# Stacked parts for the new tokens, and query/key operands made for a pair of heads: one change to a decoder-step kernel

## The chip, the core and the metric

The kernel runs on one core of one Trainium2 chip, as one program. The metric is the device time of one execution in microseconds (us), smaller is better; the figure of a kernel is the median of several executions. Engines are named as the profile names them: PE is TensorE's matmul stream and PEld its weight loads, DVE is VectorE, ACT is ScalarE, POOL is GpSimd, SP is SyncE, whose queue issues nearly all transfers.

## What is computed

One inference step of a two-layer hybrid decoder, in float32, for a prompt of 512 tokens and 64 "new" tokens (8 samples with 8 tokens each and 1024 cached keys each).

```
layer 0:  qa,ka,va,qi,ki,wi,qb,kb,vb,fb = split(h @ w_in)        # h: 512 + 64 rows of 1024
          A: per-query top-k keys by an indexer, softmax over them      (8 heads of 64)
          B: softmax with a forget gate: s + cum[t] - cum[s], causal    (8 heads of 64)
          x = LN(ALPHA*x + (1+g1) * (concat(A,B) @ w_out))
layer 1:  u, v = split(gelu(h @ w_in_c)); x = LN(ALPHA*x + (1+g1) * ((u * (W_s LN(v) + b)) @ w_out_c))
each:     h = x*(1+scale)+shift;  x = LN(ALPHA*x + (1+g2) * ConvFFN(h))
```

The prompt attends to itself; each sample attends to its cached pages, found through a page table, and to its own 8 new rows.

## The kernel before

**Split operands.** Products are made at float32 precision from float32r operands: a value is split into a high part (rounded, suffix `h`) and a low part (what is left, suffix `l`), and `mm3` adds the three products high-high, high-low and low-high. `split_to` makes a pair: a cast on ACT, then a subtraction on DVE. `weights` (L250 to L254) loads a unit of 128 x 1024 weights as `wr`, casts it to `wh` on ACT and subtracts to `wl` on DVE or POOL.

**Token-major projections.** `token_unit` computes rows of tokens times a unit of weights: for each block of 128 prompt tokens by three products (L283 to L285), and for the block of 64 new tokens (`tb` = 4) by a single plain float32 product per 128 rows of the model dimension, `xn` against the unsplit weight `wr` (L702). Even and odd `k` go into the lower and upper 64 partitions of one accumulator, and `both_halves` (L717 ACT, L718 DVE) adds the two halves. This code serves `w_ab` (2 projections, 8 units, 512 columns a product), `w_aa` (3 projections, 12 units, 256 columns) and the v half of the gMLP, `w_v` (16 units, 256 columns). `xn` is made in `modulate` (L430, a POOL copy per 128 features) for layer 0 and in `Norm.finish` (L144, L146) for the gMLP.

**Attention of the prompt.** `attend_prompt` goes through 8 heads of B and then 8 of A; a head has four steps `tb`, one for each block of 128 queries: scores (L1265, L1266, for B also L1268), softmax (`softmax`, L1201 to L1204), transposes (L1273), and a copy out (L1274). After the second head of a pair, eight products with the values follow (L1282). `operands` makes what a head needs: `qS` (scaled query; partitions 0 to 63 hold the high part, 64 to 127 the low part), `kH` and `kL` (the key's parts, twice, so that one product adds two), for B also `cq`. It loads the 64 rows of one head twice, into the lower and the upper half of a tile called `both` (L1220 for B, L1226 for A; A's rows are token-major and go through four transposes a tile, L1229). The operands of the next head are asked for at step `TA` = 1 of the present one; there are two buffers of each (`QB`), and three of `both` (`TWB`).

**What sets the order.** The code asks for the work in the order above, interleaved with generators: in the attention stage the heads advance by 1.2 steps for each step of `attend_sample`, which loads two pages at a time (L269) into the weight buffers and multiplies them (L1329 scores, L1363 values). A scheduler then places each instruction in its engine's queue. Queues run in order; SP's queue holds the page loads, the loads of `both` and `rows`, and 128 loads of page numbers (L277).

**Stages of the traced execution:** layer 0 projections with the first sample attention (0 to 366 us), attention of the prompt with the rest of the sample attention (366 to 578), output projection and ConvFFN (to about 1121), gMLP with its v projection first (1121 to 1235), the rest of layer 1.

Of the kernel before, what the change touches and what calls it, by code (L numbers as in the profile page):

```python
# [48 lines left out]
LB = 'gv'  # L49
TWB = 3  # L50
BP = 200
# [4 lines left out]
GO = (((0,4),(4,8),(8,12)),((12,16),))  # L56
QB = 2


class Norm:  # L60
# [56 lines left out]
    def finish(self, part):  # L117
# [19 lines left out]
        if part:  # L137
            ps = psum.tile([P, KB, NS], F32, name="tp", bufs=2)
            for kb in range(KB):
                nc.tensor.transpose(ps[:, kb], rt[:NS, 4, kb * P:(kb + 1) * P], ident[:NS, :NS])  # L140
            self.xn = xp.tile([P, KB, NS], F32, name="xn")
            t = self.xn.rearrange("p k (b q) -> p k b q", b=8)
            wide = lambda m: m[:, :, :, None].to_broadcast([P, KB, 8, 8])
            nc.vector.tensor_tensor(t, ps.rearrange("p k (b q) -> p k b q", b=8), wide(self.gains), op=OP.mult)  # L144
            nc.scalar.copy(x[:, :, NP:], ps)
            nc.vector.tensor_tensor(t, t, wide(self.offs), op=OP.add)  # L146
            net.split_to(*(w[:, :, NP:] for w in self.out), self.xn)
        for k0 in range(0, KB, 2):
            ks = slice(k0, k0 + 2)
# [53 lines left out]
class Net:  # L203
# [217 lines left out]
    def modulate(self, xk, sc1, sh, kb, pool):  # L421
# [126 lines left out]
    def gmlp(self, x, last, psum, pool, xp, *norm):  # L548

        nc, a, xs, xn = self.nc, self.a, last.xs, last.xn  # L550
        g1 = self.plus_one(1, 2, xp, "g1")
# [21 lines left out]
        def lead():  # L573
            c, u = todo.pop(0)
            if u == 0:
                led[c] = [], [psum.tile([P, 2, 256], F32, name=name, bufs=b) for name, b in (("acc", 4), ("tc", 2))]
            units, accs = led[c]
            units.append(self.weights(a["w_v"][c, u], 1024))
            self.token_unit({tb: accs[tb // 4][:, tb % 2] for tb in (2, 3, 4)}, units[u], u, 256, xs, xn, True, (2, 3, 4))

# [3 lines left out]
        for c in range(8):  # L584
            first = None
            for u in range(2):
# [3 lines left out]
                first = first or psum.tile([P, 2, 256], F32, name="acc", bufs=4)  # L590
                self.token_unit([first[:, 0], first[:, 1]], units[u], u, 256, xs, xn, True, (0, 1))
            accs = [first] + led.pop(c)[1]
# [91 lines left out]

    def token_unit(self, accs, w, u, n, xs, xn, shared=False, tbs=range(5), between=None):

# [4 lines left out]
        for tb in tbs:  # L691
            for j in range(per):
# [14 lines left out]
    def token_product(self, accs, srcs, xs, xn, n, between=None, shared=False, before=None):  # L707

        for u, src in enumerate(srcs):
            w = self.weights(src, 1024)  # L710
            if before:
                before(u)
            self.token_unit(accs, w, u, n, xs, xn, shared, between=between)

# [55 lines left out]
    def project(self, keep, pool, room, psum, free):  # L770
# [5 lines left out]
        xs = self.xs = [self.halves(tuple(x[:, kb] for x in self.xhl)) for kb in range(KB)]  # L776
        self.xn = pool.tile([P, KB, NS], F32, name="xn")
        self.sc1 = pool.tile([P, KB, 9], F32, name="sc1")
# [56 lines left out]
        toks = self.five(psum)  # L835
        self.token_product(toks, [a["w_ab"][0, u] for u in range(4)], xs, self.xn, 512, None, False, before)
        qit = self.pair(tmp, [P, 4, NP], "qit")
# [5 lines left out]
        kd = tmp.tile([P, 5, P], F32, name="kd")  # L843
        rt = tmp.tile([P, 5, 64], F32, name="rt8")
        for n, t0, t1 in ((P, 0, 4), (NS, 4, 5)):
# [18 lines left out]
        for ci, name in enumerate(("qi", "vb")):  # L864
            accs = toks
            if ci:
                accs = self.five(psum)
                self.token_product(accs, [a["w_ab"][ci, u] for u in range(4)], xs, self.xn, 512, between)
            for tb in range(5):
# [50 lines left out]
    def project_a(self, pool, psum, xs, between):  # L920
# [3 lines left out]
        for c, name in enumerate(("va", "ka", "qa")):  # L924
            for half in range(2):
                cols = slice(256 * half, 256 * half + 256)
                accs = [psum.tile([P, 2, 256], F32, name="s", bufs=5) for _ in range(3)]
                self.token_product([accs[tb // 2][:, tb % 2] for tb in range(5)], [a["w_aa"][c, half, u] for u in range(2)],
                                   xs, self.xn, 256, between, True)
                for i in range(3):  # L930
# [275 lines left out]

    def operands(self, kind, h, hm, pool, psum):

        nc = self.nc
        hp, par = h // 2, h % 2
        qs, kh, kl = (pool.tile([P, NP], F32R, name=n, bufs=QB) for n in ("qS", "kH", "kL"))
        low = slice(64, P)
        for c in "qk":
            t = pool.tile([P, NP], F32, name="both", bufs=TWB)
            src = self.qkv[c + kind]
            if kind == "b":
                for d in range(2):
                    nc.sync.dma_start(t[64 * d:64 * d + 64], src[hp, 64 * par:64 * par + 64])  # L1220
            else:

                rows = t.rearrange("p (t d n) -> p t d n", t=4, d=2)
                src = src.rearrange("(t p) n -> p t n", p=P)[:, :, 64 * h:64 * h + 64]
                for d in range(2):
                    nc.sync.dma_start(rows[:, :, d], src)  # L1226
                t = psum.tile([P, NP], F32, name="tp", bufs=2)
                for tb in range(4):
                    nc.tensor.transpose(t[:, tb * P:(tb + 1) * P], rows[:, tb].rearrange("p d n -> p (d n)"), self.ident)  # L1229
# [5 lines left out]
        cq = v = None  # L1235
        if kind == "b":
            cq = pool.tile([P, NP], F32R, name="cq", bufs=QB)
            nc.gpsimd.tensor_scalar(cq, self.cumq[h // 4].bitcast(F32), hm[:, h % 4:h % 4 + 1], None, op0=OP.mult)
        if par == 0:
            v = pool.tile([P, NP], F32, name="rows", bufs=2).rearrange("p (t n) -> p t n", t=4)  # L1240
            nc.sync.dma_start(v, self.qkv["v" + kind].rearrange("(t p) n -> p t n", p=P)[:, :, hp * P:hp * P + P])
        return qs, kh, kl, cq, v

    def attend_prompt(self, mt, pool, ptp, psum, flush):
# [3 lines left out]
        heads = [(kind, h) for kind in "ba" for h in range(8)]  # L1248
        ahead = [self.operands(*heads[0], hm, pool, psum)]
        for i, (kind, h) in enumerate(heads):  # L1250
# [3 lines left out]
            first = 0 if kind == "a" else 4  # L1254
            qs, kh, kl, cq, v = ahead.pop()
# [378 lines left out]
```

## Time and profile before

| | |
|---|---|
| median of 3 executions | 1940.66 us (1937.17 to 1941.69) |
| profiled execution, own time | 1944.53 us |
| its span | 1942.8 us |
| busy: PE, PEld, DVE, ACT, POOL | 94%, 84%, 60%, 38%, 18% |
| mean granted TensorE clock | 0.97 of full |
| transfers | 283.36 MB, 146 GB/s over the span |

The span is the time from the first to the last instruction; 1.7 us of the execution lie around it. A busy share is an average over stages with different limits; in PE's row of the 40 slices the digits are 8 and 9 nearly everywhere, and the DMA row has 5 to 9 in slices 4 to 12, which end with the attention of the prompt, and at most 5 after them.

### The profile page before, as it was taken

What the parts mean: (1) busy time and instruction counts of PE and PEld (TensorE: products, weight loads), DVE (VectorE), ACT (ScalarE), POOL (GpSimd) and SP (SyncE); (2) the same over time, 40 slices, a digit from 0 to 9 for tenths busy, and PEclk for the clock granted to TensorE, in tenths of its full rate; (3) what the DMA queues carried; (4) which work ended last, traced back from release to release, by engine and by line L of the source; (5) the groups of instructions that cost most, each with busy time, mean ns of one, the idle gap of its engine ahead of it and who ended that gap; (6) DMA issues with size and microseconds to landing.
All of it is one profiled execution on the core that took longest, in us unless ns stands there. A gap on an engine that the chain in (4) does not pass through costs nothing. (4 is left out here: it accounts for less than half of the span.)

```text
span 1942.8 us, 37068 instructions
## 1 busy us (share of the span) xinstructions
PE 1826.5 (94%) x14460; PEld 1622.8 (84%) x14460; DVE 1157.8 (60%) x2426; ACT 743.7 (38%) x1382; POOL 351.3 (18%) x518
## 2 busy tenths in 40 slices
PE   6889999899889899999999999999998999999996
PEld 4647877655459799999999989999997999999995
DVE  2549963465448754545556963465577655555577
ACT  2323222255443542424345432422234535344543
POOL 2323511110015310101012330110013101010124
PEclk9989999999899999999999999999998999999997
DMA  8346577797874335353543422332132222213242
GB/s 288 127 155 219 179 253 244 241 307 232 266 240 149 116 131 189 135 161 135 195 141 107 131 92 78 97 97 59 63 112 72 78 97 67 97 56 108 87 139 92
DMA packets 140865, 283.36 MB, mean 146 GB/s; under 512 B 32722, under 2 KB 43922, under 8 KB 140690
## 3 DMA queue, kind: packets, MB, share of 16 engines
q1 hardware_dynamic: 139970, 278.64, 43.9%
q0 software_dynamic: 720, 2.36, 0.5%
q8 instruction: 114, 1.87, 0.4%
q14 instruction: 61, 0.50, 0.1%
HBM read 270.00 MB, written 10.94 MB: 145 GB/s over the span
## 5 line engine op out<-in xcount | busy, mean ns | idle before, releaser
L298 PE MATMUL acc<-xl,wh 128*128 128x256 f32 (+1 forms) x1664 | 496.2, 298 | 5.9 <-DVE xl L162 5.9
L298 PE MATMUL acc<-xh,wh 128*128 128x256 f32 (+1 forms) x1664 | 498.6, 300 | 2.9 <-ACT xh L161 1.7
L298 PE MATMUL acc<-xh,wl 128*128 128x256 f32 (+1 forms) x1664 | 495.0, 298 | 0.0
L251 ACT CAST wh<-wr 128x1024 fp32r<-128x1024 f32 (+2 forms) x276 | 260.7, 949 | 537.3 <-PE acc L298 375.3
L254 DVE TENSOR_TENSOR wl<-wr,wh 128x1024 fp32r<-128x1024 f32 (+2 forms) x211 | 226.7, 1076 | 248.0 <-ACT wh L251 222.4
L298 PEld LDWEIGHTS acc<-xh,wh 128*128 128x128 f32 x1664 | 318.2, 191 | 11.7 <-issue 6.4
L298 PEld LDWEIGHTS acc<-xl,wh 128*128 128x128 f32 x1664 | 318.5, 191 | 7.5 <-DVE xl L162 7.1
L298 PEld LDWEIGHTS acc<-xh,wl 128*128 128x128 f32 x1664 | 318.5, 191 | 0.4 <-issue 0.4
L254 POOL TENSOR_TENSOR wl<-wr,wh 128x1024 fp32r<-128x1024 f32 x65 | 160.9, 2476 | 526.6 <-ACT wh L251 471.8
L298 PE MATMUL acc<-gl,wh 128*128 128x256 f32 (+1 forms) x704 | 209.5, 299 | 0.0
L298 PE MATMUL acc<-gh,wl 128*128 128x256 f32 (+1 forms) x704 | 207.8, 298 | 1.6 <-DVE wl L254 1.6
L298 PE MATMUL acc<-gh,wh 128*128 128x256 f32 (+1 forms) x704 | 208.2, 301 | 0.4 <-ACT gh L760 0.4
L439 DVE SCALAR_TENSOR_TENSOR x<-acc,g,x 128x256 f32<-128x256 f32 x256 | 119.7, 476 | 116.9 <-PE acc L298 111.5
L525 DVE SCALAR_TENSOR_TENSOR y<-up,wc,y 128x592 f32<-128x592 f32 x176 | 150.6, 856 | 34.0 <-ACT y L522 30.0
L298 PEld LDWEIGHTS acc<-gh,wh 128*128 128x128 f32 x704 | 132.9, 190 | 5.5 <-ACT wh L251 2.1
L298 PEld LDWEIGHTS acc<-gh,wl 128*128 128x128 f32 x704 | 132.8, 190 | 2.9 <-DVE wl L254 1.9
L298 PEld LDWEIGHTS acc<-gl,wh 128*128 128x128 f32 x704 | 133.9, 190 | 0.3 <-DVE gl L761 0.2
L518 POOL COPY tail<-up 128x2 f32<-128x2 f32 x88 | 26.3, 299 | 519.1 <-ACT up L516 518.8
L516 ACT COPY up<-acc 128x256 f32<-128x256 f32 x176 | 65.2, 371 | 129.9 <-PE acc L298 121.7
L283 PE MATMUL s<-wh,xh 128*128 128x256 f32 (+1 forms) x256 | 81.7, 327 | 1.4 <-ACT wh L251 1.4
L522 ACT ACTIVATE y<-up,wc 128x592 f32<-128x592 f32 x88 | 77.8, 884 | 9.2 <-POOL up L514 1.1
L285 PE MATMUL s<-wh,xl 128*128 128x256 f32 (+1 forms) x256 | 81.3, 317 | 0.0
(442 smaller groups left out, 3468.3 us busy)
## 6 DMA issues: line engine op xcount, KB each, us to landing
wr<-in_w_up SPq DMA_DIRECT2D x88, 512.0 KB
wr<-in_w_down SPq DMA_DIRECT2D x32, 512.0 KB
wh<-in_w_mod SPq DMA_DIRECT2D x30, 512.0 KB
wl<-in_w_mod SPq DMA_DIRECT2D x30, 512.0 KB
wr<-in_w_mod SPq DMA_DIRECT2D x28, 512.0 KB
own<-in_kT_b SPq DMA_DIRECT2D x48, 256.0 KB
own<-in_v_b SPq DMA_DIRECT2D x44, 256.0 KB
wr<-in_w_down SPq DMA_DIRECT2D x32, 320.0 KB
```

Of the source, the lines that this page charges most:

```text
L251: nc.scalar.copy(h, r)
L254: (nc.vector if low == "v" else nc.gpsimd).tensor_sub(l, r, h.bitcast(F32))
L283: mm(out, sh, mh, start=start, stop=False)
L285: mm(out, sl, mh, start=False, stop=stop)
L298: mm(acc, w[:, k * P:(k + 1) * P], m, start=i == 0, stop=i == n - 1)
L439: nc.vector.scalar_tensor_tensor(xp, acc[:, :256], g1[:, ob, 0:1], xp, op0=OP.mult, op1=OP.add)
L516: nc.scalar.copy(u[:, 2 + 256 * part:258 + 256 * part], accs[part][:, :256])
L518: nc.gpsimd.tensor_copy(tail[:, blk, 0:2], u[:, NP:NP + 2])
L522: nc.scalar.activation(y[:, :n], u[:, 0:n], AF.Identity, bias=wc[:, 3, blk:blk + 1], scale=wc[:, 0, blk:blk + 1])
L525: nc.vector.scalar_tensor_tensor(y[:, :n], u[:, k:k + n], wc[:, k, blk:blk + 1], y[:, :n], op0=OP.mult, op1=OP.add)
```

## The change

Two edits, and some buffer counts.

1. **New tokens.** `xn` is replaced by `xst`, which holds for each `k` the high and the low part of the 64 new tokens side by side, 128 columns in all. A product with `wh` and one with `wl` (L707 of the new file) replace the plain product with `wr`: partitions 0 to 63 of the accumulator collect the high rows, 64 to 127 the low rows, and `both_halves` adds them as it did. `xst` is filled by POOL copies from the split operands: two per 128 features in `modulate`, and two of 128 x 512 in each of the three norms that have a next layer (only the one before the gMLP is read).
2. **Operands by pair.** `operands` is called once for a pair of heads, at step 0 of the pair's second head. It loads the 128 rows of both heads once for the query and once for the key, transposes them once (A), and then makes each head's `qS`, `kH` and `kL` from 64 rows at a time. `QB` is 3, `TWB` is 2.

```diff
-        nc.gpsimd.tensor_copy(self.xn[:, kb], t[:, NP:])
         self.split_to(*(x[:, kb] for x in self.xhl), t)
+        for i, x in enumerate(self.xhl):
+            nc.gpsimd.tensor_copy(self.xst[:, kb, i], x[:, kb, NP:])
...
             net.split_to(*(w[:, :, NP:] for w in self.out), self.xn)
+            self.xst = xp.tile([P, KB, 2, NS], F32R, name="xst")
+            for i, w in enumerate(self.out):
+                nc.gpsimd.tensor_copy(self.xst[:, :, i], w[:, :, NP:])
...
-                    c = 64 * (k % 2)
-                    self.nc.tensor.matmul(accs[tb][c:c + NS], xn[:, k], wk[2], start=k < 2, stop=k >= KB - 2,
-                                          tile_position=(0, c))
+                    x = xst[:, k].rearrange("p i n -> p (i n)")
+                    for i in range(2):
+                        self.nc.tensor.matmul(accs[tb], x, wk[i], start=k + i == 0, stop=k + i == KB)
...
-            if kind == "b":
-                for d in range(2):
-                    nc.sync.dma_start(t[64 * d:64 * d + 64], src[hp, 64 * par:64 * par + 64])
+            if kind == "b":
+                nc.sync.dma_start(t, src[hp])
             else:
-                rows = t.rearrange("p (t d n) -> p t d n", t=4, d=2)
-                src = src.rearrange("(t p) n -> p t n", p=P)[:, :, 64 * h:64 * h + 64]
-                for d in range(2):
-                    nc.sync.dma_start(rows[:, :, d], src)
+                rows = t.rearrange("p (t n) -> p t n", t=4)
+                nc.sync.dma_start(rows, src.rearrange("(t p) n -> p t n", p=P)[:, :, hp * P:hp * P + P])
...
-            if c == "q":
-                nc.scalar.activation(qs, t, AF.Copy, scale=0.125)
-                nc.vector.scalar_tensor_tensor(qs[low], t[low], 0.125, qs[low].bitcast(F32), op0=OP.mult, op1=OP.subtract)
-            else:
-                self.split_to(kh, kl, t)
+        for (qs, kh, kl), own in zip(ops, halves):
+            nc.scalar.activation(qs[:64], tq[own], AF.Copy, scale=0.125)
+            nc.vector.scalar_tensor_tensor(qs[low], tq[own], 0.125, qs[:64].bitcast(F32), op0=OP.mult, op1=OP.subtract)
+            for half in halves:
+                nc.scalar.copy(kh[half], tk[own])
+                nc.vector.tensor_sub(kl[half], tk[own], kh[half].bitcast(F32))
...
-                if tb == TA and i < 15:
-                    ahead.append(self.operands(*heads[i + 1], hm, pool, psum))
+                if tb == 0 and par and i < 15:
+                    kind2, h2 = heads[i + 1]
+                    ahead += self.operands(kind2, h2 // 2, hm, pool, psum)
```

The order moves at three places that matter below. Line numbers of the new file are 3 to 6 higher for the same code.

PE before, at the end of one unit of the gMLP's v projection (`acc` are prompt tokens, `tc` holds the new tokens):

```order
L284 MATMUL acc<-wl,xh 128x256
L285 MATMUL acc<-wh,xl 128x256
L702 MATMUL tc<-wr,xn 64x256 x4
L283 MATMUL acc<-wh,xh 128x256
L284 MATMUL acc<-wl,xh 128x256
```

and PE now, at the same place:

```order
L287 MATMUL acc<-wl,xh 128x256
L288 MATMUL acc<-wh,xl 128x256
L707 MATMUL tc<-wh,xst 128x256
L707 MATMUL tc<-wl,xst 128x256
L707 MATMUL tc<-wh,xst 128x256
L707 MATMUL tc<-wl,xst 128x256
L707 MATMUL tc<-wh,xst 128x256
L707 MATMUL tc<-wl,xst 128x256
L707 MATMUL tc<-wh,xst 128x256
L707 MATMUL tc<-wl,xst 128x256
L286 MATMUL acc<-wh,xh 128x256
L287 MATMUL acc<-wl,xh 128x256
```

Four plain products become eight float32r products, in the same place between the same neighbours.

DVE before, early in the A heads, ahead of a `mtl` (the low part of a pair's result; `selp` is the mask of the selected keys, `p` the probabilities, `mx` the sample attention's maximum):

```order
L1201 ISA p,nm<-s,selp_1223 128x512
L1201 ISA nm 128x1
L1203 RECIPROCAL sm<-sm 128x1
L1204 TENSOR_SCALAR p<-p,sm 128x384
L1232 SCALAR_TENSOR_TENSOR qS<-tp,qS 64x512
L1203 RECIPROCAL sm<-sm 128x1
L1204 TENSOR_SCALAR p<-p,sm 128x512
L761 TENSOR_TENSOR mtl<-o,mth 128x512
```

and DVE now, around the same `mtl`:

```order
L1208 TENSOR_SCALAR p<-p,sm 128x384
L1235 SCALAR_TENSOR_TENSOR qS<-tp,qS 64x512
L1338 TENSOR_REDUCE mx<-s 128x1
L1238 TENSOR_TENSOR kL<-tp,kH 64x512
L1235 SCALAR_TENSOR_TENSOR qS<-tp,qS 64x512
L1238 TENSOR_TENSOR kL<-tp,kH 64x512
L765 TENSOR_TENSOR mtl<-o,mth 128x512
L1238 TENSOR_TENSOR kL<-tp,kH 64x512
L1338 TENSOR_REDUCE mx<-s 128x1
L1205 ISA p,nm<-s,selp_1245 128x512
L1205 ISA nm 128x1
L1238 TENSOR_TENSOR kL<-tp,kH 64x512
```

The softmax over four blocks (128x512) stood ahead of the operand instruction there; now five of a pair's six operand instructions stand ahead of it.

SP before, at the first operands of the attention stage (`d_qb`, `o_bk_p`, `o_bv_p` are the stored queries, keys and values of B):

```order
L1220 DMA both<-d_qb 64x512 x2
L1220 DMA both<-o_bk_p 64x512 x2
L1241 DMA rows<-o_bv_p 128x4x128
L944 DMA d_qa<-ro 128x2x256
L1220 DMA both<-d_qb 64x512 x2
```

and SP now:

```order
L1224 DMA both<-d_qb 128x512
L1224 DMA both<-o_bk_p 128x512
L1246 DMA rows<-o_bv_p 128x4x128 x2
L1224 DMA both<-d_qb 128x512
```

Pairs of half-tile loads become single loads; the first of them now stands behind ten further page loads (eight of keys, two of values) that stood after it.

## Rows read from the trace of the kernel before

**Rows 1.** Windows: PE, PEld, DVE, ACT, POOL busy; PEclk, DMA share, GB/s

```profile
300.00:372.00 72.00, 64.56 (x710) 50.71 (x708) 25.32 (x62) 14.72 (x35) 11.03 (x9) 0.95 0.72 236
...
366.00:578.00 212.00, 177.47 (x1712) 106.58 (x1704) 110.27 (x372) 104.19 (x294) 19.75 (x18) 0.92 0.85 261
...
1121.00:1235.00 114.00, 113.45 (x891) 101.07 (x892) 53.92 (x108) 37.35 (x60) 15.68 (x13) 0.99 0.29 95
```

**Rows 2.** Timeline of PE in the gMLP: start us, duration us, instruction

```profile
1181.92 0.28 PE L284 MATMUL acc<-wl,xh 128*128 128x256 f32 x1
1182.04 0.28 PE L285 MATMUL acc<-wh,xl 128*128 128x256 f32 x1
1182.25 1.08 PE L702 MATMUL tc<-wr,xn 128*64 128x256 f32 x8
...
1183.49 0.28 PE L284 MATMUL acc<-wl,xh 128*128 128x256 f32 x1
```

**Rows 3.** Timeline of PE around one unit of `w_ab`

```profile
59.78 0.39 PE L284 MATMUL s<-wl,xh 128*128 128x512 f32 x1
60.02 0.40 PE L285 MATMUL s<-wh,xl 128*128 128x512 f32 x1
60.34 1.08 PE L702 MATMUL s<-wr,xn 128*64 128x512 f32 x4
61.35 0.35 PE L283 MATMUL tp<-xh,cums 128*80 128x256 f32 x1
```

**Rows 4.** Timeline of PE around one unit of `w_aa`

```profile
364.75 1.08 PE L702 MATMUL s<-wr,xn 128*64 128x256 f32 x8
365.76 0.64 PE L1363 MATMUL o<-wr,ptS 128*32 128x128 f32 x16
```

**Rows 5.** Source L430 (ns min/median/max, starts), and a POOL timeline row

```profile
L430 POOL COPY xn<-tmp x8: 237/238/239, 14.6 to 59.0; 128x64 f32<-128x64 f32 x8
...
94.09 0.54 POOL L1016 MEMSET rt<- 128x512 f32 x1
```

**Rows 6.** Timelines of POOL and DVE at the norm before the gMLP

```profile
1108.37 2.40 POOL L254 TENSOR_TENSOR wl<-wr,wh 128x1024 fp32r<-128x1024 f32 x1 [3.33 <-ACT wh L251]
...
1108.85 2.47 DVE L162 TENSOR_TENSOR xl<-tmp,xh 128x512 fp32r<-128x512 f32 x1
...
1122.64 0.68 DVE L162 TENSOR_TENSOR xl<-tmp,xh 128x512 fp32r<-128x512 f32 x1
```

**Rows 7.** Timeline of PE: transposes of one A head's operands

```profile
459.20 1.09 PE L1229 MATMUL tp<-c_ident,both 128*128 128x128 f32 x8
460.22 0.62 PE L1329 MATMUL s<-wl,qbda 128*32 128x256 f32 x2
```

**Rows 8.** Waits of PE, 372 to 580 us: total us, times, longest

```profile
PE tp L1353 <- ACT pS L1344: 6.5, 4, 2.1
PE s L1329 <- DMA wr<-in_kT_a: 5.7, 3, 3.7
PE s L1265 <- DVE qS L1232: 2.9, 1, 2.9
PE s L1329 <- DMA wh<-in_kT_a: 2.3, 1, 2.3
```

**Rows 9.** Lines, 366 to 578 us: busy us, mean ns | idle before, releaser

```profile
L1232 DVE SCALAR_TENSOR_TENSOR qS<-both,qS 64x512 fp32r<-64x512 f32 x8 | 5.9, 736 | 4.3 <-ACT qS L1231 4.0
L761 DVE TENSOR_TENSOR kL<-tp,kH 128x512 fp32r<-128x512 f32 x8 | 5.5, 690 | 2.7 <-ACT kH L760 2.7
...
L760 ACT CAST kH<-both 128x512 fp32r<-128x512 f32 x8 | 4.9, 619 | 7.2 <-DMA both<-o_bk_p 6.9 <-PE s L1266 0.3
```

**Rows 10.** Transfers of 370 to 580 us, and one of the issue rows

```profile
DMA packets 47615, 54.38 MB, mean 259 GB/s; under 512 B 20087, under 2 KB 24439, under 8 KB 47588
...
both<-d_qa SPq DMA_DIRECT2D x16, 128.0 KB
```

**Rows 11.** Issue of the loads of `both` on SP: ns min/median/max

```profile
L1220 SPq DMA_DIRECT2D both<-d_qb x16: 451/460/1287, 366.4 to 425.4; - x16
```

More of the change, by code (lines that the diff above doesn't have):

```diff
@@ L548, in gmlp @@
     def gmlp(self, x, last, psum, pool, xp, *norm):
-        nc, a, xs, xn = self.nc, self.a, last.xs, last.xn
+        nc, a, xs, xst = self.nc, self.a, last.xs, last.xst
         g1 = self.plus_one(1, 2, xp, "g1")
@@ L578, in lead @@
             units.append(self.weights(a["w_v"][c, u], 1024))
-            self.token_unit({tb: accs[tb // 4][:, tb % 2] for tb in (2, 3, 4)}, units[u], u, 256, xs, xn, True, (2, 3, 4))
+            self.token_unit({tb: accs[tb // 4][:, tb % 2] for tb in (2, 3, 4)}, units[u], u, 256, xs, xst, True, (2, 3, 4))
         for _ in range(3):
@@ L590, in gmlp @@
                 first = first or psum.tile([P, 2, 256], F32, name="acc", bufs=4)
-                self.token_unit([first[:, 0], first[:, 1]], units[u], u, 256, xs, xn, True, (0, 1))
+                self.token_unit([first[:, 0], first[:, 1]], units[u], u, 256, xs, xst, True, (0, 1))
             accs = [first] + led.pop(c)[1]
@@ L683, in rows, with token_unit @@
         return bass.AP(tensor=ap.tensor, offset=ap.offset, ap=[[0, n]] + [list(s) for s in ap.ap[1:]])
-    def token_unit(self, accs, w, u, n, xs, xn, shared=False, tbs=range(5), between=None):
+    def token_unit(self, accs, w, u, n, xs, xst, shared=False, tbs=range(5), between=None):
         per = 1024 // n
@@ L712, in token_product @@
                 before(u)
-            self.token_unit(accs, w, u, n, xs, xn, shared, between=between)
+            self.token_unit(accs, w, u, n, xs, xst, shared, between=between)
     def both_halves(self, acc, out):
@@ L776, in project @@
         xs = self.xs = [self.halves(tuple(x[:, kb] for x in self.xhl)) for kb in range(KB)]
-        self.xn = pool.tile([P, KB, NS], F32, name="xn")
+        self.xst = pool.tile([P, KB, 2, NS], F32R, name="xst")
         self.sc1 = pool.tile([P, KB, 9], F32, name="sc1")
@@ L835, in project @@
         toks = self.five(psum)
-        self.token_product(toks, [a["w_ab"][0, u] for u in range(4)], xs, self.xn, 512, None, False, before)
+        self.token_product(toks, [a["w_ab"][0, u] for u in range(4)], xs, self.xst, 512, None, False, before)
         qit = self.pair(tmp, [P, 4, NP], "qit")
@@ L867, in project @@
                 accs = self.five(psum)
-                self.token_product(accs, [a["w_ab"][ci, u] for u in range(4)], xs, self.xn, 512, between)
+                self.token_product(accs, [a["w_ab"][ci, u] for u in range(4)], xs, self.xst, 512, between)
             for tb in range(5):
@@ L928, in project_a @@
                 self.token_product([accs[tb // 2][:, tb % 2] for tb in range(5)], [a["w_aa"][c, half, u] for u in range(2)],
-                                   xs, self.xn, 256, between, True)
+                                   xs, self.xst, 256, between, True)
                 for i in range(3):
@@ L1205, in softmax, with operands @@
         return p
-    def operands(self, kind, h, hm, pool, psum):
+    def operands(self, kind, hp, hm, pool, psum):
         nc = self.nc
-        hp, par = h // 2, h % 2
-        qs, kh, kl = (pool.tile([P, NP], F32R, name=n, bufs=QB) for n in ("qS", "kH", "kL"))
         low = slice(64, P)
+        halves = [slice(64 * par, 64 * par + 64) for par in range(2)]
+        ops = [tuple(pool.tile([P, NP], F32R, name=n, bufs=QB) for n in ("qS", "kH", "kL")) for _ in range(2)]
+        both = []
         for c in "qk":
@@ L1235, in operands @@
-        cq = v = None
-        if kind == "b":
[L1237 to L1242, printed above, removed]
+                    nc.tensor.transpose(t[:, tb * P:(tb + 1) * P], rows[:, tb], self.ident)
@@ new lines, in operands @@
+            both.append(t)
+        tq, tk = both
+        for (qs, kh, kl), own in zip(ops, halves):
[4 more added lines that the diff above has]
+                nc.vector.tensor_sub(kl[half], tk[own], kh[half].bitcast(F32))
+        cqs = [None, None]
+        if kind == "b":
+            for par in range(2):
+                h = 2 * hp + par
+                cqs[par] = pool.tile([P, NP], F32R, name="cq", bufs=QB)
+                nc.gpsimd.tensor_scalar(cqs[par], self.cumq[h // 4].bitcast(F32), hm[:, h % 4:h % 4 + 1], None, op0=OP.mult)
@@ L1244, in attend_prompt @@
+        v = pool.tile([P, NP], F32, name="rows", bufs=2).rearrange("p (t n) -> p t n", t=4)
+        nc.sync.dma_start(v, self.qkv["v" + kind].rearrange("(t p) n -> p t n", p=P)[:, :, hp * P:hp * P + P])
+        return [(*op, cq, v) for op, cq in zip(ops, cqs)]
     def attend_prompt(self, mt, pool, ptp, psum, flush):
@@ L1248, in attend_prompt @@
         heads = [(kind, h) for kind in "ba" for h in range(8)]
-        ahead = [self.operands(*heads[0], hm, pool, psum)]
+        ahead = self.operands("b", 0, hm, pool, psum)
         for i, (kind, h) in enumerate(heads):
@@ L1254, in attend_prompt @@
             first = 0 if kind == "a" else 4
-            qs, kh, kl, cq, v = ahead.pop()
+            qs, kh, kl, cq, v = ahead.pop(0)
             if par == 0:
```

9 lines of the change are left out of this document (4 added, 5 removed).

## Prediction

> **What bounds the kernel now.** I read the busy line and the 40 slices first: PE is busy 94% of the span, so the first question for each edit is how much PE time it takes away, and the second is where PE is not full. The windows answer it [rows 1]. In the gMLP's v projection (1121 to 1235 us) PE is busy 113.45 of 114 us, and the transfers use 0.29 of their time: whatever PE saves there shortens the execution. At the end of the layer 0 projections (300 to 372 us) PE is busy 64.56 of 72 us, or 0.90. In the attention of the prompt (366 to 578 us) it is busy 177.47 of 212 us; the transfers are at 0.85, DVE and ACT at about half. There no engine is full: 34.5 us of PE are idle. The list of waits [rows 8] says for what: pages of the sample attention (5.7 and 2.3 us), its softmax (6.5 us), and once the first operands (2.9 us). The rest is in many small waits. So the new-token edit is a sum of PE durations, and the pair edit is a question of which of four half-loaded resources sets the pace.
>
> **New tokens, gMLP.** In the timeline [rows 2] the float32r products start 0.12 us apart (1181.92, 1182.04). From the last of these before the plain products to the second after them (1182.04 to 1183.49) 1.45 us pass, of which two steps of 0.12 would be spent without the plain ones: they cost 1.21 us a unit. The order puts eight float32r products of the same 128x256 shape in their place, 8 x 0.12 = 0.96 us. That saves 0.25 us in each of 16 units, 4.0 us, all of it on a full PE.
>
> **New tokens, layer 0.** For `w_ab` [rows 3] a step of 512 columns takes 0.24 us (59.78 to 60.02), and from 60.02 to 61.35 1.33 us pass: 1.09 us for the plain products, against 4 x 0.24 = 0.96 now. 8 units save 1.0 us. For `w_aa` between products of the sample attention [rows 4] the plain ones take 1.01 us and save 0.05; between float32r neighbours, as in rows 2, they save 0.25. Most of the 12 units stand between such neighbours in both orders, so I take 0.2: 2.4 us. PE was 0.90 busy there, so of 3.4 us I count 3.0; bounds are 0 (a wait fills it) and 4.0 (12 at 0.25, and 1.0).
>
> **New tokens, the copies.** `xst` adds 8 POOL copies to the first 8, 0.24 us each [rows 5], and they now wait for the low part, one DVE instruction later. POOL's weight subtractions are queued behind them, 8 x 0.24 = 1.9 us at most. At the three norms there are two copies of 128x512 each; the trace has none, the nearest row of that size is a fill of 0.54 us [rows 5]. Six of them are 3.2 us of POOL, which is busy for 18% of the span. I take +0.5 us, since PE has other products at both places; bounds 0 and +5.1.
>
> Here the trace has something that speaks against the change: beside a POOL subtraction of 2.40 us a DVE subtraction took 2.47 us, and 0.68 us when POOL was idle [rows 6]. The Trainium skill's "SBUF — State Buffer", section "Who interferes with whom", says that a VectorE instruction with two SBUF inputs and a GpSimd instruction that reads SBUF exclude each other for the whole instruction; the row agrees. By that rule each norm copy may hold DVE for its own length, and the sum would carry +3.2 instead of +0.5, 2.7 us more than I forecast. I keep +0.5, since in the norms PE has other products to do while DVE catches up.
>
> **Pair operands, PE.** The eight transposes of an A head take 1.02 us (459.20 to 460.22) [rows 7]. Eight heads need 64, four pairs need 32: 4.1 us of PE less. PE is 84% busy in this stage, so this could also vanish in idle time; bounds 0 and -4.1, I take all of it, since the transposes stand among the sample attention's products, which are ready.
>
> **Pair operands, transfers and SP.** In 370 to 580 us 54.38 MB move at 259 GB/s [rows 10], and 60 loads of `both` of 128 KB (16 and 16 for A, 14 and 14 for B) are 7.9 MB of it. A pair's load is half of that: 3.9 MB less, 15 us of transfer at that rate. On SP 60 issues of about 0.46 us [rows 11] become 15 or 16, so some 20 us of the queue go too, and page loads stand behind fewer others. Not all of that is time: PE waits for pages 8.0 us by the two longest rows [rows 8]. I take three quarters of it, -6 us. Bounds: 0 (the pages wait for buffers that PE frees, and none comes sooner) and -15. Against it, SP now issues the first operands behind ten more page loads: 128x512 floats each, 2.6 MB in all, 10 us at 259 GB/s if the products that come first can't use the wait. Those pages are wanted by the products beside them, so I count nothing; the first wait of 2.9 us [rows 8] may double.
>
> **Pair operands, ACT and DVE.** An instruction on 64 partitions takes as long as one on 128 (0.74 us for the `qS` subtraction on 64, 0.69 us for `kL` on 128, [rows 9]). A head had two casts on ACT and two subtractions on DVE; now it has three of each. Over 16 heads that is 16 x 0.62 = 9.9 us of ACT and 16 x 0.70 = 11.2 us of DVE, on engines with about 100 us idle in the stage. They come bunched: six on DVE for a pair, 4.2 us, where two of 1.4 us in all stood before, and a softmax of the running head stands behind them, and behind that its transposes on PE. Bounds: 0, and 8 pairs x 2.8 = 22 us if every bunch is exposed. PE has the sample attention to do meanwhile, so I take +2.5.
>
> **Buffers.** With `QB` = 3 the next pair needs two sets while the present second head holds one, so no operand waits for a buffer; `both` at 2 holds one pair's query and key, freed about 13 us (four steps of 212/64 us) ahead of the next use. I count nothing.
>
> **Sum.** -4.0 - 3.0 + 0.5 - 4.1 - 6 + 2.5 = -14.1 us. Against the profiled execution's own 1944.53 us (its span of 1942.8 and 1.7 around it) that is 1930.4. That execution is 3.9 us above the median of the three that were timed, so I forecast 1926.5 us for a median.
>
> **Rivals.**
> - *The attention stage keeps its length.* PE's 34.5 idle us absorb what is taken out, and the bunches on ACT and DVE take the rest. For it: PE is idle for its own softmax chain (6.5 us in rows 8) as much as for pages. Against it: 0.85 of the transfer time is used. Then only -6.5 is left: 1934.
> - *The transfers set the pace of that stage.* Its full 15 us come off, with the transposes and the projections: -15 - 4.1 - 6.5 + 2.5 = -23, or 1917.5. For it: the share is 0.85 on average, and one slice of the stage shows 9 tenths. Against it: PE waits for pages only 8.0 us in the two rows.
> - *Slower: DVE's bunches hold up the softmax.* The price is up to 22 us at eight pair boundaries; the other terms without +2.5 give -16.6, so this decides from 2.1 us a boundary on, and at full price the time is 1940.66 - 16.6 + 22 = 1946. For it: the order above, where a softmax stands behind five operand instructions. Against it: DVE is 52% busy, and PE has other products there.
>
> **How the numbers follow.** Forecast 0.45, attention unchanged 0.22, transfers 0.18, bunches 0.15. The forecast's own range is 1919 to 1934, from half to one and a half times the terms of the attention stage. The 8-in-10 range takes in the first two rivals and the smaller half of the third: 1912 to 1941. A measurement of this kernel tells about 0.2%, 3.9 us, from no change, so faster means below 1936.8: nearly all of the forecast (0.44), three quarters of the first rival (0.16) and the second (0.18) make 0.78. Between 1936.8 and 1944.5 lie the rest of the first and a quarter of the third, 0.10; slower is 0.12.
>
> **What would show it.** In the gMLP's v window, 16 groups of L707 of eight products and about 0.96 us each, and the stage 4 us shorter; if the groups take over 1.1 us, the first step is wrong. In the attention stage: 32 operand transposes instead of 64; about 50.5 MB moved; the waits of PE for `kT_a` at 2 us or less; the stage near 205 us. Waits of PE for `p` or of the transposes L1273 for DVE that grow by 10 us or more would show the bunches. A first score product (L1265 of before) for which PE waits much longer than 2.9 us would show the SP order as the cost.

## The result and the profile after

The changed kernel took 1927.89 us (median of 5 runs, 1925.89 to 1930.81) against 1939.15 us of the kernel before beside it: ratio 0.9937, interval 0.992 to 0.9953. A second group of runs gave 1929.35 us (6 runs) against 1941.07 (17 runs of before beside them): 0.9934, interval 0.9915 to 0.9952. The forecast was 1926.5 us. As a change, -14.1 us was forecast and -11.3 and -11.7 were measured. So the total came out near the forecast; the parts did not, and this section and the next two are about that. In the last group of runs one of 24 executions of before took 3684.76 us, and it is left out everywhere.

The windows of the changed kernel, for the stages of [rows 1] (columns as there):

```profile
300.00:372.00 72.00, 64.11 (x740) 55.14 (x738) 27.69 (x66) 15.85 (x36) 11.25 (x12) 0.97 0.76 253
361.00:566.50 205.50, 169.87 (x1684) 107.16 (x1683) 124.36 (x391) 116.69 (x310) 20.24 (x18) 0.91 0.73 249
1108.00:1219.30 111.30, 108.67 (x889) 107.98 (x890) 54.93 (x106) 36.73 (x59) 15.59 (x13) 0.99 0.27 87
```

In the attention stage PE's busy time fell from 177.47 to 169.87 us, DVE's rose from 110.27 to 124.36 and ACT's from 104.19 to 116.69, and the transfers' share fell from 0.85 to 0.73. PE's idle time stayed: 34.5 us before, 35.6 after. In the gMLP's v projection PE, which was nearly full before (113.45 of 114 us), is now idle for 2.6 us. One unit of the gMLP, on PE's timeline (answers to [rows 2]):

```profile
1168.46 0.28 PE L288 MATMUL acc<-wh,xl 128*128 128x256 f32 x1
1168.58 0.28 PE L707 MATMUL tc<-wh,xst 128*128 128x256 f32 x1
1168.70 0.28 PE L707 MATMUL tc<-wl,xst 128*128 128x256 f32 x1
...
1169.42 0.28 PE L707 MATMUL tc<-wl,xst 128*128 128x256 f32 x1
1169.54 0.28 PE L286 MATMUL acc<-wh,xh 128*128 128x256 f32 x1
```

The eight products take 1168.58 to 1169.54, 0.96 us, to the hundredth what was counted. PE's waits in 361 to 566.5 us (total us, times, longest; answers to [rows 8]):

```profile
PE s L1271 <- ACT kH L1237: 13.2, 3, 9.2
PE s L1271 <- DVE nm L1205: 3.5, 4, 1.8
PE tp L745 <- DVE ro L732: 3.2, 1, 3.2
PE tp L1359 <- ACT pS L1350: 3.0, 4, 1.3
```

The waits for `kT_a` pages are gone from the list (8.0 us by two rows of [rows 8]). At its head stands a new one: the first score product (L1271) waits 9.2 us for ACT's first `kH` cast. What lies before that cast is on SyncE's queue:

```profile
365.87 0.86 SPq L272 DMA_DIRECT2D wr<-in_kT_b  x2
366.97 0.85 SPq L272 DMA_DIRECT2D wh<-in_v_b  x2
367.87 0.53 SPq L240 DMA_DIRECT2D i_c_tri<-in_c_tri  x1
369.04 0.34 SPq L240 DMA_DIRECT2D i_c_hm<-in_c_hm  x1
369.69 0.33 SPq L1224 DMA_DIRECT2D both<-d_qb  x1
370.35 0.33 SPq L1224 DMA_DIRECT2D both<-o_bk_p  x1
```

and on PE's timeline, with the idle time ahead of each in brackets:

```profile
367.46 0.48 PE L745 MATMUL tp<-c_ident,ro 64*128 64x64 f32 x2 [3.24 <-DVE ro L732]
377.12 0.47 PE L1271 MATMUL s<-kH,qS 128*128 128x128 f32 x1 [9.18 <-ACT kH L1237]
377.53 1.06 PE L1335 MATMUL s<-wl,qbdb 128*32 128x256 f32 x2
```

The first load is issued at 369.69 us, behind the pages (before: 366.4, [rows 11]), and PE's score products begin at 377.12 (374.2 before). The products on the pages (L1335) start right behind the first score product, without a wait of their own. This long wait is the sign that the prediction named for the order on SP as the cost. The pair's instructions, by shape (columns as in [rows 9]):

```profile
L1238 DVE TENSOR_TENSOR kL<-both,kH 64x512 fp32r<-64x512 f32 x16 | 12.5, 784 | 6.2 <-ACT kH L1237 5.7
...
L1237 ACT CAST kH<-both 64x512 fp32r<-64x512 f32 x16 | 9.9, 616 | 6.4 <-DMA both<-o_bk_p 4.8 <-PE s L1271 1.3
...
L1230 PE MATMUL tp<-c_ident,both 128*128 128x128 f32 x32 | 4.7, 280 | 0.7 <-DVE outal L765 0.7
```

32 transposes stand where there were 64, and a cast of 64 partitions (616 ns) costs what one of 128 did (619 ns in [rows 9]). The copies into `xst` in `modulate` (columns as in [rows 5]):

```profile
L435 POOL CAST xst<-xh x8: 760/822/827, 15.3 to 59.3; 128x64 fp32r<-128x64 f32 x8
L435 POOL CAST xst<-xl x8: 231/235/488, 16.8 to 60.2; 128x64 fp32r<-128x64 f32 x8
```

The copies of the high part take 0.82 us, and each runs beside a DVE subtraction (L765); those of the low part take 0.24 us, mostly with no DVE instruction beside them. The transfers of 361 to 567 us, beside [rows 10]:

```profile
DMA packets 34492, 51.37 MB, mean 249 GB/s; under 512 B 3162, under 2 KB 11866, under 8 KB 34466
```

### The profile page after: what moved, and what is told of

The parts are those of the page before. It is cut to its first block, busy times and chain, and to the rows that moved or that the text cites. A ratio compares the mean times of both kernels' runs of the same rounds, so it can differ in the third digit from the quotient of the medians.

```text
span 1927.3 us, 36981 instructions
## 1 busy us (share of the span) xinstructions
PE 1811.6 (94%) x14428; PEld 1641.9 (85%) x14428; DVE 1171.3 (61%) x2442; ACT 755.8 (39%) x1398; POOL 363.2 (19%) x532
## 5 line engine op out<-in xcount | busy, mean ns | idle before, releaser
L522 POOL COPY tail<-up 128x2 f32<-128x2 f32 x88 | 26.8, 305 | 519.2 <-ACT up L520 518.9
L287 PE MATMUL s<-wl,xh 128*128 128x256 f32 (+1 forms) x256 | 81.3, 318 | 0.0
```

What stands on the lines that cost most here:

```text
L287: mm(out, sh, ml, start=False, stop=False)
L522: nc.gpsimd.tensor_copy(tail[:, blk, 0:2], u[:, NP:NP + 2])
```

## The experiments

The kernels were timed in four groups, each beside its own runs of the kernel before, whose medians were 1939.15 us (5 runs, group 0), 1943.37 (11, group 1), 1941.07 (17, group 2) and 1941.13 (23, group 3). The column "less before" is a kernel's median less that of its own group; the ratio with its interval is taken inside the group too, but not from the medians. Differences between kernels of different groups below are differences of that column, with the plain difference of the medians beside them; where the two disagree by 2 us or more, so much is uncertain. For the stages I read five marks in each profiled execution: the start of the last new-token product of layer 0 (T), of the first score product of the prompt (S), of the last output product of the prompt (O), and of the first and last new-token product of the gMLP (V1, V2).

| kernel (group) | median us (runs) | less before | ratio, interval | T | S | O | V1 | V2 | span |
|---|---|---|---|---|---|---|---|---|---|
| before, profile above (0) | 1939.15 (5) | | 1 | 365.4 | 374.2 | 576.3 | 1121.8 | 1231.6 | 1942.8 |
| before, again (2) | 1932.80 (1) | | | 360.6 | 368.5 | 564.5 | 1110.0 | 1219.8 | 1931.0 |
| changed (0) | 1927.89 (5) | -11.3 | 0.992-0.9953 | 361.1 | 377.1 | 564.8 | 1108.0 | 1216.5 | 1927.3 |
| changed, again (2) | 1929.35 (6) | -11.7 | 0.9915-0.9952 | 361.3 | 377.8 | 567.4 | 1110.7 | 1219.3 | 1930.2 |
| tokens alone (1) | 1929.39 (6) | -14.0 | 0.9894-0.9937 | 361.6 | 370.6 | 564.6 | 1110.0 | 1217.0 | 1928.7 |
| pair alone (1) | 1932.00 (5) | -11.4 | 0.9925-0.9959 | 361.8 | 378.1 | 569.3 | 1114.1 | 1223.9 | 1932.4 |
| first loads early (1) | 1914.95 (4) | -28.4 | 0.9835-0.9872 | 360.8 | 368.3 | 554.3 | 1098.7 | 1205.8 | 1913.6 |
| shared loads, head by head (1) | 1934.06 (5) | -9.3 | 0.9931-0.9966 | 360.6 | 370.1 | 574.2 | 1121.7 | 1228.7 | 1937.7 |
| same, loads as before (2) | 1940.68 (12) | -0.4 | 0.9975-1.0008 | 357.1 | 366.7 | 570.3 | 1116.5 | 1223.5 | 1933.1 |
| tokens, first loads early (2) | 1928.58 (6) | -12.5 | 0.9913-0.9954 | 360.8 | 362.4 | 557.5 | 1109.1 | 1216.6 | 1925.1 |
| rt line alone (3) | 1945.37 (12) | +4.2 | 1.0006-1.0035 | 361.1 | 368.9 | 572.8 | 1121.7 | 1231.6 | 1942.4 |
| transposes twice (3) | 1929.51 (7) | -11.6 | 0.9917-0.9962 | 357.9 | 373.2 | 561.1 | 1105.9 | 1212.9 | 1923.9 |
| casts twice (3) | 1940.17 (12) | -1.0 | 0.997-0.9996 | 358.4 | 376.4 | 578.1 | 1122.8 | 1231.3 | 1939.1 |
| early, fewer copies (3) | 1911.79 (5) | -29.3 | 0.9818-0.9859 | 360.8 | 367.8 | 553.0 | 1097.3 | 1204.3 | 1912.2 |

**The kernel before, again.** No edit.

> The kernel before once more, for a second profile: how far the stage marks of one and the same program move from one execution to another. In the first profile the layer-0 projections' last new-token product starts at 365.4 us, the attention stage from there to its last output product takes 210.9 us. Theory A, that the 365.4 is what the plain product costs: within 1 us again. Theory B, that the marks move with the execution (the pair edit alone, with the same plain product, has it at 361.8): 361 to 364.

Theory B: the same program moved by 11.8 us, all of it ahead of O; from O to the end both executions took 1366.5 us, and the changed kernel's two agree as well, 1362.5 and 1362.8. Its attention stage:

```profile
361.00:565.00 204.00, 177.03 (x1714) 107.85 (x1712) 109.32 (x370) 103.81 (x294) 19.97 (x18) 0.92 0.87 269
```

PE's busy time is that of [rows 1] (177), the stage 8 us shorter. So a mark ahead of O tells little from a single profile: it can be off by some 5 to 10 us, and there the medians count. From O to the end one program repeats to 0.3 us, but a new order can move this stretch too: it took 1369.6 us in "rt line alone", which changes nothing there. This also says that the profile on which I predicted was one of the longer executions.

**Each edit alone.** The token edit: the changed kernel with the operand code and ring sizes of before.

```diff
-    def operands(self, kind, hp, hm, pool, psum):
+    def operands(self, kind, h, hm, pool, psum):
...
-TWB = 2
+TWB = 3
...
-QB = 3
+QB = 2
```

> The new-token edit alone (stacked xst, two float32r products in place of one plain one); queries and keys are loaded and made head by head as before. My theory: the two edits add up, and this one is worth the 4.3 us of the layer-0 projections plus 1.8 us of the gMLP v stage seen between the two traces: about 6 us less than before (ratio 0.997). Rival, that the tokens' gain is absorbed at the next waits: ratio 0.999 to 1.000. Rival, that what was won behind the attention stage (13.6 us at the gMLP's first product against 11.5 at the attention stage's end) comes from the tokens' kernel order: 8 us.

The pair edit is the other half: the kernel before with the new operands, rings and `rt` line, and the plain product.

> The pair edit alone (operands loaded once a pair and made at the first step of the second head, rings of 3 and 2); the new tokens go through the plain product as before. My theory: 7 us less than before in the attention stage (-4.1 transposes, -6 transfers, +2.5 bunches by the prediction; 7.2 in the trace), ratio 0.996. Rival, that the stage keeps its length and the gain came with the tokens: ratio 0.999 to 1.001. Rival, that the transfers were worth more than the whole of it and the bunches cost the difference, isn't told apart by this run but by the one that makes the operands head by head.

Medians: 14.0 us less than before for the tokens, 11.4 for the pair, 11.3 and 11.7 for both. My theory that they add is refuted; each edit alone gave more than I expected (6 and 7 us), the tokens about twice as much, and beside them the pair edit gave nothing.

**The changed kernel, again.**

> The changed kernel once more, timed beside the same runs of the kernel before as the other kernels of this group, so that the parts can be compared with the whole on one chip. The edits alone gave ratios 0.9916 and 0.9942 to before, which would multiply to 0.986. Theory that they add: ratio 0.986 to 0.988. Theory that both remove the same waits in part and that the late first operands of the pair edit (9 us) take back what it wins: 0.992 to 0.995, as at first.

0.9934: not the sum. Why the two gains overlap no run shows.

**First loads early.** The first pair's loads go to a weight tile, asked for before the first page of the stage.

```diff
+            w = net.raw()
+            ahead = net.operands("b", 0, hm, att, psum, [w[:, :NP], w[:, NP:]])
...
-            t = pool.tile([P, NP], F32, name="both", bufs=TWB)
+            t = own.pop(0) if own else pool.tile([P, NP], F32, name="both", bufs=TWB)
```

> The changed kernel, but the first pair's query and key loads go into one of the weight tiles and are issued ahead of the page loads, so that they have long landed when the projections end; all else as changed. In the changed kernel TensorE sits 9.2 us for the first kH cast, since SyncE issues those loads at 369.7 us, behind ten page loads. Theory that the attention stage's length is counted from its first score product: the first product starts 7 to 9 us earlier (about 368 us), and the time falls by 5 to 9 us against the changed kernel (1919 to 1923 us, ratio to before 0.990 to 0.992). Rival, that the stage is paced by ACT, DVE or the transfers so that a later start is made up: less than 1.5 us.

1914.95 us: 28.4 less than before where the changed kernel is 11.7 less, so 16.7 faster than it (14.4 by the plain medians), more than the 5 to 9 expected. The scheduler put the loads at 314 us (count, ns min/median/max, first and last start, of SyncE):

```profile
L1224 SPq DMA_DIRECT2D wr<-d_qb x1: 371/371/371, 314.0 to 314.0; - x1
L1224 SPq DMA_DIRECT2D wr<-o_bk_p x1: 422/422/422, 314.4 to 314.4; - x1
```

and PE's first score product came 8.8 us sooner:

```profile
365.97 0.34 PE L745 MATMUL tp<-c_ident,ro 64*128 64x64 f32 x2 [2.10 <-DVE ro L732]
368.34 0.48 PE L1268 MATMUL s<-kH,qS 128*128 128x128 f32 x1 [2.03 <-ACT kH L1237]
```

By the marks 8.8 to 9.5 us of the gain are the earlier start, 1.7 to 3.6 lie between S and O and 3.2 to 3.5 behind O. The start is the edit; the rest came with it, presumably by the order of the instructions, and no run separates it.

**Tokens, first loads early.** The same edit on the kernel with the token edit alone.

> The token edit alone (operands made head by head as before), but with the first head's query and key loads into a weight tile, issued ahead of the page loads, as in the kernel whose first pair is loaded early. Against that one only the pair edit differs, its late start taken out of both. Theory that the pair edit is worth 6 to 8 us inside the attention stage once its first operands are there: this kernel 6 to 8 us slower than it (ratio 0.989), and 1 to 3 us faster than the token edit alone, whose first score product waits 2.7 us. Rival, that the early loads make the whole difference and the pair edit none: as fast as it, 0.985.

Neither: the first product came 8.2 us sooner, O 7.1 us sooner, and the execution gained nothing: 12.5 us less than before, against 14.0 without the early loads (0.8 us shorter by the plain medians). From O to V1 it took 551.6 us where the kernel with the pair edit and early loads took 544.4. With both loads early the pair edit is worth 15.9 us (13.6 by the plain medians). In the two profiles 3.2 of it are there at O, and 8.3 appear behind it, where neither edit has attention code. That part I can't settle. It limits what the run before this one says: a start about 9 us sooner gained 14 to 17 us there, and a start 8.2 us sooner gained nothing here.

**Shared loads, head by head**, and the same **with the loads of before**. They split the pair edit. In the first a pair's tiles are loaded once, but each head's operands are made at the second step of the head before, with the changed kernel's 64-partition instructions and 64 transposes. In the second each head's half is loaded twice, as before.

```diff
-                if par == 0:
-                    nc.sync.dma_start(t, src[hp])
+                for d in range(2):
+                    nc.sync.dma_start(t[64 * d:64 * d + 64], src[hp, 64 * par:64 * par + 64])
...
```

> The changed kernel, but only the loads are shared by a pair: the operands are made head by head at the second step of the head before, as in the kernel before (transposes of the second kind of attention 64 as before, rings of 2 and 3 as before). It parts the pair edit in two: against the kernel with the token edit alone only the transfers and SyncE's issues differ (and the 64-partition ACT and DVE instructions), against the changed kernel only the transposes and the bunching. By the prediction's terms: 6 us faster than the token edit alone, 1.6 us slower than the changed kernel (+4.1 transposes, -2.5 bunches), about 1929 to 1930 us. Rival A, transfers were hidden: as slow as the token edit alone (about 1933 to 1935). Rival B, transfers set the pace and bunches cost: as fast as the changed kernel or faster, 1922 to 1927.

> As the kernel that shares the loads and makes the operands head by head, with the same 64-partition ACT and DVE instructions at the same places, but the loads are again the kernel before's: each head's half loaded twice, into both halves of its tile (eight transfers a pair in place of two, some 4 MB more). Only the transfers and SyncE's issues differ between the two. By the prediction's term for the transfers: 6 us slower than with shared loads (about 0.998 to before). Rival, transfers hidden: within 1.5 us of it (0.995). Rival, transfers set the pace: 10 us slower or more (1.000).

The kernel with shared loads misses its expectation: it was to be 6 us faster than the tokens alone, and is 4.7 us slower beside them in the same group (1934.06 and 1929.39). Its time falls on the figure of rival A (1933 to 1935), but that rival had the tokens alone there too. Against the kernel that differs in the loads alone it is faster by 8.9 us (9.3 and 0.4 less than before; 6.6 by the plain medians, 1934.06 and 1940.68), with intervals apart: the loads are worth what the prediction's term says or somewhat more, and the rival of 10 us isn't excluded. (The two profiled executions lie at the other ends of their ranges and don't show it.) What moved in their attention stages, loads of before first, then shared:

```profile
DMA packets 48416, 55.58 MB, mean 266 GB/s; under 512 B 20307, under 2 KB 24773, under 8 KB 48388
```

```profile
DMA packets 35091, 52.65 MB, mean 247 GB/s; under 512 B 3229, under 2 KB 11933, under 8 KB 35064
```

Against the tokens alone the kernel with the loads of before is 13.6 us slower (11.3 by the plain medians). It issues the same loads and makes the operands at the same step; what it has more is 16 ACT and 16 DVE instructions.

**Transposes twice.**

```diff
-                for tb in range(4):
+                for tb in (0, 0, 1, 1, 2, 2, 3, 3):
                     nc.tensor.transpose(t[:, tb * P:(tb + 1) * P], rows[:, tb], self.ident)
```

> The changed kernel, with each operand transpose of the second kind of attention done twice into the same place: 64 as in the kernel before, 32 more than in the changed one, all else unchanged. By the prediction's term (1.02 us per 8, all on TensorE's path): 4.1 us slower than the changed kernel, about 1933 us, ratio 0.9955. Rival, that they fall into TensorE's 34 idle us of the stage: within 1 us of the changed kernel (0.9935).

1929.51 us against 1929.35, and 11.6 against 11.7 less than before: the rival. The transposes are there,

```profile
L1230 PE MATMUL tp<-c_ident,both 128*128 128x128 f32 x64 | 8.3, 278 | 0.0
```

and S to O took 187.9 us, where the changed kernel's two profiles have 187.7 and 189.6. By this 32 transposes fall into PE's idle time; but the intervals allow 4 us or more, the size of the term itself.

**Casts twice.**

```diff
-            for half in halves:
+            for half in halves + halves:
                 nc.scalar.copy(kh[half], tk[own])
                 nc.vector.tensor_sub(kl[half], tk[own], kh[half].bitcast(F32))
```

> The changed kernel, with the key casts on ACT and the low-part subtractions on DVE done twice for each head (64 more ACT instructions of about 0.62 us and 64 more DVE ones of about 0.70 us in the bunches, 40 and 45 us of the two engines). It prices the bunches: by the prediction's term (2.5 us for 22 us of added DVE and ACT work) some 7 us slower than the changed kernel and 10 us at most. Rival, that bunches are exposed on the softmax chain: 30 us or more. Rival, that they are hidden: under 2 us, apart from the first pair's, where TensorE waits for the first casts (about 2.6 us more).

My count was wrong there: the edit adds 32 instructions to each engine, not 64, some 20 and 22 us. They cost 10.8 us (1.0 and 11.7 less than before), and S to O took 201.7 us. PE's waits in 361 to 579 us:

```profile
PE s L1271 <- ACT kH L1237: 14.3, 5, 11.3
PE tp L1279 <- ACT pt L1280: 6.6, 7, 2.4
PE tp L1279 <- DVE qS L1235: 3.5, 2, 2.2
PE tp L1279 <- ACT wh L254: 3.3, 1, 3.3
```

2 us more for the first cast, and PE now waits for ACT and DVE at the softmax's transposes (L1279): the cost is half of the added DVE time, though both engines are idle for a third of the stage.

**The rt line alone.** The change also takes a scratch tile of the key rotation from another ring.

```diff
-        rt = tmp.tile([P, 5, 64], F32, name="rt8")
+        rt = pool.tile([P, 512], F32, name="rt", bufs=2)[:, :320].rearrange("p (t d) -> p t d", t=5)
```

> The kernel before with one line of the change alone: the scratch tile of the layer-0 key rotation (kd's rt, 128x5x64) taken from the ring of two rt tiles of 512 in the kept pool, in place of a tile of its own in the temporary pool. Nothing else changes; it removes no instruction. The prediction gave it no term. The token edit alone (9 us less than the kernel before up to the last attention product, by the medians) and the pair edit alone (6 us less) both hold this line, and together they gave 8. Theory that the line itself moves the order of work in the first 570 us and is what the two share: ratio 0.995 to 0.997. Rival, that it does nothing: 0.999 to 1.001, and the overlap of the two edits has another cause.

Neither: 4 us slower than before, with no instruction added. It is not what the two edits share. It suggests how much a new order alone can do here.

**Early, fewer copies.** First loads early, and `xst` copied only at the norm whose result is read by `xst`.

```diff
-            for i, w in enumerate(self.out):
+            for i, w in enumerate(self.out if self.nxt == (1, 0) else ()):
```

> The kernel with the first pair's loads early, and with the xst copies at the norms left out where nothing reads them (two of the three norms). It prices the dead copies of the change: by the prediction's term at the norms (a part of +0.5 us) 0 to 1 us faster than with the loads alone (ratio 0.985). Rival, that POOL's dead copies delay the low parts behind them: 2 to 4 us faster.

1911.79 us: 0.9 us better than with the early loads alone in the column, 3.2 by the plain medians, with intervals that overlap, so the medians don't tell theory from rival. Of the 1.4 us between the two profiles 1.3 lie ahead of O, where the edit has no code. At the norm behind it, where POOL's two copies took 0.89 and 0.66 us, the two profiles differ by 0.3 us at most, as in the theory. It is the fastest version: 1.6% below before, about 1% below the changed kernel.

## Why the prediction came out right

The total was near by luck: several steps were wrong, and their errors went both ways. By its steps:

- **New tokens, gMLP, -4.0: right in price, only in part in effect.** 0.96 us a group, as counted. The column chunks of two units, by the starts of the `z` copies, follow each other every 13.44 us once the stage runs evenly, 13.91 before: 0.23 a unit, 3.7 for 16. But V1 to V2 shortened by only 1.3 us, and by 2.8 in the kernel with this edit alone, where the granted clock of the stretch was 1.00 (0.98 before, 0.99 in the changed kernel). "All of it on a full PE" is what failed: in the first units PE is now ahead of the norm and waits 2.6 us for its parts (1.9 for `xl`, 0.7 for `xh`). In V1 to V2 PE is idle for 2.1 to 2.7 us in all ten profiles with the stacked product and for 0.0 in all four with the plain one. The stretch from O to the end doesn't price the product: it is 3.7 to 4.0 us shorter with both edits, 2.4 with the tokens alone, and 3.4 with the pair alone, which has the plain product.
- **New tokens, layer 0, -3.0: fits, not shown.** T is at 360.6 to 365.4 in four executions with the plain product (mean 362.2) and at 357.1 to 361.6 in ten with the stacked one (mean 360.0): 2.2 us, in ranges that overlap.
- **The copies, +0.5: right at a norm**, 0.3 at the one where it could be read. In `modulate` they were taken at 0.24 us each, but those of the high part took 0.82 us beside DVE's subtraction, so POOL got some 6.6 us more there and not 1.9; what that cost PE no run shows. The price of 2.7 us more, by the Trainium skill's "SBUF — State Buffer", section "Who interferes with whom", did not show at that norm.
- **Transposes, -4.1: not borne out.** "I take all of it, since the transposes stand among the sample attention's products, which are ready." Doing them twice cost 0.2 us in the medians, though the intervals allow 4 or more. PE's busy time fell by 7.6 us in the stage, and against the second execution of before idle time took its place (26.8 us of T to O there, 34.2 now).
- **Transfers and SP, -6: right in size or somewhat small**, 6.6 to 8.9 by the pair of kernels that differ in nothing else; and the page waits went, as the test said.
- **ACT and DVE, +2.5: too small.** Twice the addition cost 10.8 us, so an estimate of half of it is 5.4; made head by head just ahead of use it cost 11.3 to 13.6. How long ahead of their use the instructions are issued seems to matter too: the changed kernel, which makes the operands up to a head sooner, is 2.4 to 4.7 us faster than the one head by head, in spite of a start 6.5 us later (S less T 16.0 and 9.5). But it has half the transposes as well, and the intervals overlap.
- **First operands, counted at nothing: wrong, and the largest miss.** "Those pages are wanted by the products beside them, so I count nothing." The products on those pages stand behind the first score product in PE's order, and PE ran none of them in its 9.18 idle us. S less T grew from 8.8 and 7.9 us to 16.0 and 16.5: 7 to 9 us. Ending the wait gave 14 to 17 us beside the pair edit and nothing beside the tokens alone, so its price in the total isn't known better than that.
- **Not in the sum:** the tokens alone gave 14.0 us (11.8 by the plain medians) and not 6.5, and the runs don't show why. The token edit moved SyncE's operand loads among the page loads in the attention stage, where it has no code, so the order may be the cause; but T to O took 203.0 us there and 210.9 and 203.9 in the two executions of before, so a single profile doesn't show a gain. The granted clock of this stretch is a rival that no run separates: 0.94 with the tokens alone, 0.92 in both executions of before, 0.91 and 0.90 in the changed kernel's two.

Added up, these measurements come to between -1 and +4 us. The tokens' unexplained part takes off another 7 to 11, which makes -12 to -3. The measured -11.3 and -11.7 lie at the edge of that, and most of them is the part that no run explains: the account is not closed. The forecast's range was also said to be "half to one and a half times the terms of the attention stage"; these terms (-7.6) would give 1923 to 1930, and 1919 to 1934 is half to one and a half times the whole sum.

The rungs, each less its own before: tokens -14.0; with the 64-partition instructions -0.4; with shared loads -9.3; with the pair made ahead, and half the transposes, -11.7. From the first on, the pair edit's own gains and costs are +13.6, -8.9 and -2.4 (+11.3, -6.6 and -4.7 by the plain medians): about nothing. The rival "attention keeps its length" (1934 us) was right about the stage once the tokens are in, and wrong about the total, since the tokens gave more than their products.

## What to carry to other kernels

A busy share doesn't price an instruction: 32 transposes more on PE, idle for a sixth of the stage, cost 0.2 us (known to some 4), and 32 casts and 32 subtractions more on ACT and DVE, idle for a third, cost 10.8. A faster step counts only while its inputs keep up. Look for the instruction that stands at the head of an engine's queue: a load that was issued 3 us later, and 7 to 8 later against the end of the projections, left PE idle for 9.2 us with other products behind it. Make operands in few, wide instructions: 64 partitions cost what 128 do (616 and 619 ns). Profile the same program twice before reading a difference of 10 us out of two profiles, compare a kernel with the runs of before beside it, and price every line of a change, also one that removes no instruction.

## What was not expected of the hardware

One program's executions spread over 12.5 us here (1937.1 to 1949.7 in 23 runs of before, and 1932.8 in the second profiled one), and the mean granted clock moved with it (0.964 in the slowest, 0.975 in the fastest; 1.0 us less for each 0.001 more by a straight line through the 23; which of the two moves the other no run shows). All of the 11.8 us between two profiles lay in the first 565 us, where the transfers are at 0.4 to 1.0 of their time; the 1366.5 us behind took the same to a tenth. A line that only moved a scratch tile shifted the median by 4 us.
